# Layer-norm lo parts and sums of u moved to VectorE, the last token tile finished later, and layer norm ranked ahead of weight splits

## The chip, the core and the metric

The kernel runs on one core of a Trainium2 chip. The metric is the device time of one launch in microseconds (us). The core has five engines that each work through a fixed list of instructions in order: TensorE (matmuls and transposes; PE in the profile, its weight loads PEld), VectorE (DVE), ScalarE (ACT), GpSimd (POOL) and SyncE (SP, which issues the DMAs here). They wait for one another through semaphores.

## The reference, cut to what matters

One inference step of a two-layer backbone for 128 context tokens and 512 latent tokens of width 1024. Each layer has three sublayers, and each sublayer ends in a layer norm; the modulated input of the next one is u.

```python
def swiglu(u, lp, j):
    return (jax.nn.silu(u @ lp['ffn_w_gate'][j]) * (u @ lp['ffn_w_up'][j])) @ lp['ffn_w_down'][j]

def trunk_layer(x, cond, lp, ropes, ctx):
    mod = (jax.nn.silu(cond) @ lp['w_mod'] + lp['b_mod'])[:, None, :]
    sh1, sc1, g1, sh2, sc2, g2, sh3, sc3, g3 = jnp.split(mod, N_MOD, axis=-1)
    x = layer_norm(ALPHA * x + 0.5 * g1 * swiglu(x * (1 + sc1) + sh1, lp, 0), lp['ln_g'][0], lp['ln_b'][0])
    y, ctx_out = mixer(x * (1 + sc2) + sh2, lp, ropes, ctx)      # RG-LRU, GQA and MLA heads on one input projection
    x = layer_norm(ALPHA * x + g2 * y, lp['ln_g'][1], lp['ln_b'][1])
    x = layer_norm(ALPHA * x + 0.5 * g3 * swiglu(x * (1 + sc3) + sh3, lp, 1), lp['ln_g'][2], lp['ln_b'][2])
    return x, ctx_out
```

All is float32; D_FF is 2816.

## The kernel before

**Numbers as pairs.** A float32 matmul is made of three matmuls in the faster fp32r type: every operand is split into a hi part (a rounded copy, made by ScalarE) and a lo part (the rest, a subtraction). Weights are split as they come: `weight` returns a load and two splits, hi (L195, ScalarE) and lo (L200, VectorE). `mm3` (L537 to L539) issues the three matmuls.

**Phases.** The 640 tokens are five tiles of 128 (tile 0 is the context). The phases in order: FFN 0 of layer 0 (`ffn_steps`), mixer, FFN 1 (`ffn_fast`), then layer 1: FFN 0 (`ffn_fast`), mixer, FFN 1 (`ffn_fast`). So there are five layer ends inside the kernel and a last one at its end. The first phase, which computes u in another way, isn't touched by the change, except at its layer end.

**A layer end.** The last down projection (L832 or L1203 to L1205) or the output projection of the mixer goes tile by tile. VectorE multiplies each half tile from PSUM with the gate, adds it to x and takes the statistics (`ln_part`, L478). `end_tile` calls `ln_a` for the tile (aggregate L485, +eps L487, the power -0.5 on GpSimd L488, the offset L502, then the normalization in place, one part on ScalarE L506 and the rest on VectorE L508), and, one tile later, `modulate`, which calls `ln_b`: eight transposes on TensorE (L516), the evacuation with scale and shift into `uf` (L521 on VectorE, L523 on ScalarE), the hi part of u on ScalarE (L527) and its lo part on GpSimd (L529). The last tile's `ln_b` is kept in `after_q` and issued by `after_a`, which the next phase's `first` calls once the matmuls of its first weight on the first 384 tokens (24, tiles 0 to 2) are issued.

**The start of a fast FFN.** `first` of `ffn_fast` does block m = 0: gate on tokens 0 to 383, then `after_a`, up on the same tokens, gate and up on the other tokens. Blocks m = 1 and 2 follow in the same way, in halves of 320 tokens. Meanwhile `sums` forms the sums of quarters of u that the later blocks use (a Strassen scheme of seven products, L1091): eight additions hi + lo on GpSimd (`whole`, L990), then additions (L997, L1002, L1003, L1009) and splits (L985, L986) on VectorE and ScalarE. `third` follows, and hands PSUM over to the banks of the seven products, once the evacuations of block m = 2 (`hout`, L941, and `split_h`, L926) are through. `residual` (L2351, L2352) rescales x for the next sublayer at the same time, on VectorE.

**The order.** The framework plans each engine's list ahead of time: at each moment the instruction of the highest rank among those that are ready by its plan; rank is program order, and `high_priority(offset=n)` moves what is inside n places ahead (AHEAD is 100, SUMS is 200). On the chip the lists stand as planned. `run` issues a step's own splits before its body, and, between the pieces of its body, splits of the next steps: of the first `look` steps that have any, `cap` of them at most.

```python
            near = [todo[k] for k in range(i + 1, min(len(steps), i + 40)) if steps[k].splits][: s.look]
            cap = s.cap
            for more in s.body():
                cap += more or 0
                nxt = next((q for q in near if q), None)
                if nxt and cap and self.ahead and nxt[0].ready():
                    nxt.popleft()()
                    cap -= 1
```

A split is ready once its load has been issued; seven raw buffers (NR) limit how far loads run ahead. The steps of `tokens` (four column blocks of the mixer's input projection, two weights with four splits each) have a cap of 2; the last of them adds 2 in its body. Between them and their neighbours stand `proj` steps with two splits.

Of the kernel before, what the change touches and what calls it, by code (L numbers as in the profile page):

```python
# [18 lines left out]
P = 128  # L19
# [5 lines left out]
CUT = 384  # L25
# [44 lines left out]
LN_LAG = 1, 1  # L70
WOUT = (0,), (1,), (2, 3)
WCAP = 1
LOV = ()
FA = 1
FIN = ()
QP = 1
# [6 lines left out]
AHEAD = 100  # L83
# [5 lines left out]
def f(ap):  # L89
    return ap.bitcast(F32)  # L90
# [20 lines left out]
class Kern:  # L111
# [359 lines left out]
            self.gb.append(t)  # L471

    def ln_part(self, t, h, n):

        if h == 0:
            self.st[t] = self.tiny([P, 4, 6], "bnst", 6)[:, 0:n]
        w = D // n
        self.nc.vector.bn_stats(self.st[t][:, h, :], self.x[t][:, h * w : (h + 1) * w])  # L478

    def ln_a(self, t):  # L480

        nc = self.nc
        x = self.x[t]
        mv = self.tiny([P, 2], "bnmv", 3)
        nc.vector.bn_aggr(mv, self.st.pop(t))  # L485
        ve = self.tiny([P, 3], "bnve", 3)
        nc.vector.tensor_scalar_add(ve[:, 0:1], mv[:, 1:2], EPS)  # L487
        nc.gpsimd.tensor_tensor(out=ve[:, 1:2], in0=ve[:, 0:1], in1=self.mhalf[:, 0:1], op=ALU.pow)  # L488
        if self.next_mod is None and t == NT - 1:
            for h in range(2):  # L490
                cs = slice(h * 512, (h + 1) * 512)
                nc.vector.scalar_tensor_tensor(  # L492
                    x[:, cs], x[:, cs], mv[:, 0:1], self.gb[0][:, cs], op0=ALU.subtract, op1=ALU.mult
                )
            for h in range(2):
                cs = slice(h * 512, (h + 1) * 512)
                nc.vector.scalar_tensor_tensor(  # L497
                    x[:, cs], x[:, cs], ve[:, 1:2], self.gb[1][:, cs], op0=ALU.mult, op1=ALU.add
                )
                nc.sync.dma_start(out=self.O[1][0, (t - 1) * P : t * P, cs], in_=x[:, cs])  # L500
            return
        nc.vector.tensor_scalar(ve[:, 2:3], mv[:, 0:1], ve[:, 1:2], -1.0, op0=ALU.mult, op1=ALU.mult)  # L502
        c = NORM_ACT[self.ln_idx[1] != 1]
        if self.next_mod is None:
            c = D
        nc.scalar.activation(x[:, 0:c], x[:, 0:c], AF.Identity, bias=ve[:, 2:3], scale=ve[:, 1:2])  # L506
        if c < D:
            nc.vector.tensor_scalar(x[:, c:D], x[:, c:D], ve[:, 1:2], ve[:, 2:3], op0=ALU.mult, op1=ALU.add)  # L508

    def ln_b(self, x, t, sp, bp, uh, ul):  # L510

        nc = self.nc
        g = 1 if t == 0 else 0
        pt = self.p2().rearrange("p a (b c) -> p (a b) c", c=P)
        for k in range(KT):
            nc.tensor.transpose(pt[:, k, :], x[:, k * P : (k + 1) * P], self.ident)  # L516
        uf = self.pp.tile([P, KT, P], F32, tag="uf", bufs=1, name=self.nm("uf"))
        for k in range(KT):
            s1, s2 = sp[:, g, k : k + 1], bp[:, g, k : k + 1]
            if k % 4 < EVAC[self.ln_idx[1] != 1]:  # L520
                nc.vector.tensor_scalar(uf[:, k, :], pt[:, k, :], s1, s2, op0=ALU.mult, op1=ALU.add)  # L521
            else:
                nc.scalar.activation(uf[:, k, :], pt[:, k, :], AF.Identity, bias=s2, scale=s1)  # L523
        for h in range(2):
            d = uh[h][:, :, t * P : (t + 1) * P]
            v = uf[:, 4 * h : 4 * h + 4, :]
            nc.scalar.copy(d, v)  # L527
            e = nc.vector if (t, h) in LOV else nc.gpsimd
            e.tensor_sub(ul[h][:, :, t * P : (t + 1) * P], v, f(d))  # L529

    def u_alloc(self):
        return [self.U([P, 4, TOK]) for _ in range(2)], [self.U([P, 4, TOK]) for _ in range(2)]
# [350 lines left out]
    def ffn_fast(self, l, j, mods):  # L883
# [8 lines left out]
        nc, I = self.nc, self.I  # L892
        env = {}
# [10 lines left out]
        def T():  # L904
            return env["pool"].tile([P, 512], F32, tag="T", bufs=2, name=self.nm("t"))
# [24 lines left out]
        def plain(m):  # L930
            g, u = {}, {}
            gl, gsp = self.weight(view(I["ffn_w_gate"], m), [P, KT, P], g, self.W)
            ul, usp = self.weight(view(I["ffn_w_up"], m), [P, KT, P], u, self.W)

            def silu(cut):
                for a, b in self.chunks(g["s"], g["ps"], cut):
                    nc.scalar.activation(a, b, AF.Silu)

            def hout(cut):
                for a, b in self.chunks(g["s"], u["ps"], cut):  # L940
                    nc.vector.tensor_mul(a, a, b)  # L941
                split_h(m, g["s"])

            def first():
                env["cm"] = self.tc.tile_pool(name=f"ffn{l}{j}", bufs=1, reuse_waits="tile")
                env["pool"] = env["cm"].__enter__()
                g["ps"], u["ps"] = self.p2(), self.p2()
                g["s"] = B()
                yield from self.mtile(g["ps"], g, 0, CUT)
                self.hold = True  # L950
                self.after_a()
                yield from self.mtile(u["ps"], u, 0, CUT)
                yield from self.mtile(g["ps"], g, 1, CUT)
                silu(CUT)
                env["sums"] = sums()
                self.bg.append(env["sums"])
                yield from self.mtile(u["ps"], u, 1, CUT)
                hout(CUT)

            def gate():  # L960
                g["ps"] = self.p2()
                g["s"] = B()
                for c in range(2):
                    yield from self.mtile(g["ps"], g, c)
                silu(HALF)

            def up():
                u["ps"] = self.p2()
                for c in range(2):
                    yield from self.mtile(u["ps"], u, c)  # L970
                hout(HALF)

            if m == 0:
                return [Step([gl, ul], gsp + usp, first)]
            return [Step([gl], gsp, gate), Step([ul], usp, up)]


        def sums():
            uh, ul = self.uh, self.ul
            env["S"] = {i: (SB([P, 4, HALF]), SB([P, 4, HALF])) for i in (1, 2, 4)}  # L980
            env["s3"] = []

            def put(i, t, ks):
                hi, lo = env["S"][i]
                nc.scalar.copy(hi[:, ks], t)  # L985
                nc.vector.tensor_sub(lo[:, ks], t, f(hi[:, ks]))  # L986

            def whole(h, ts, ks):
                t = B().rearrange("p (k n) -> p k n", k=2)
                nc.gpsimd.tensor_add(t, f(uh[h][:, ks, ts]), f(ul[h][:, ks, ts]))  # L990
                return t

            for r in range(2):
                ks = slice(2 * r, 2 * r + 2)
                with self.tc.high_priority(offset=SUMS):
                    t21, t22 = whole(0, H1, ks), whole(1, H1, ks)
                    nc.vector.tensor_add(t22, t21, t22)  # L997
                yield
                with self.tc.high_priority(offset=SUMS):
                    t11 = whole(0, H0, ks)  # L1000
                    put(1, t22, ks)
                    nc.vector.tensor_sub(t21, t11, t21)  # L1002
                    nc.vector.tensor_sub(t11, t22, t11)  # L1003
                yield
                env["s3"].append((t21, ks))
                with self.tc.high_priority(offset=SUMS):
                    t12 = whole(1, H0, ks)
                    put(2, t11, ks)
                    nc.vector.tensor_sub(t12, t12, t11)  # L1009
                    put(4, t12, ks)  # L1010
                yield
# [168 lines left out]
        def down(ms, begin=False, last=False):  # L1180
            def body():
# [12 lines left out]
                for t in range(NT):  # L1194
                    x = acc[t]
                    ts = slice(t * P, (t + 1) * P)
                    for h in range(2):
                        pt = self.p1()
                        cs = slice(h * 512, (h + 1) * 512)
                        for i, m in enumerate(ms):  # L1200
                            hh, hl = hs[m]
                            d = dws[m]
# [3 lines left out]
                        if begin:  # L1206
                            with self.tc.high_priority(offset=AHEAD):
                                nc.scalar.copy(x[:, cs], pt)
                        elif last:
                            tt = T()  # L1210
                            nc.vector.tensor_mul(tt, pt, env["gate"][1 if t == 0 else 0][:, cs])
                            nc.vector.tensor_add(x[:, cs], x[:, cs], tt)
                            self.ln_part(t, h, 2)
                        else:
                            with self.tc.high_priority(offset=AHEAD):
                                nc.vector.tensor_add(x[:, cs], x[:, cs], pt)  # L1216
# [80 lines left out]
    def mixer_steps(self, l, mods):  # L1297
        nc, I, O = self.nc, self.I, self.O
        env = {}
# [796 lines left out]
        def tokens(c0, evac, post, pre=lambda: None, pairs=0):  # L2096
# [39 lines left out]
                post()  # L2136
                yield

            return Step(lds, sps, body, 2)

        def kv_evac(t, pt):
            if t == 0:
# [444 lines left out]
```

## Time and profile before

| | us |
|---|---|
| median of 3 runs (lowest to highest) | 2592.18 (2592.03 to 2599.52) |
| profiled execution, its own time | 2593.82 |
| profiled execution, span of the trace | 2592.0 |
| TensorE busy in it | 2470.4 |
| VectorE busy in it | 1887.8 |
| ScalarE busy in it | 1067.8 |
| GpSimd busy in it | 534.6 |

The span runs from the first to the last instruction of the profiled execution; the 1.8 us between it and that execution's time lie around it. Busy times are sums of what the engines execute; time in which an engine waits is idle. The granted clock of TensorE is given as a share of its full 2.4 GHz; over the whole execution it was 0.984.

### The profile page before, as it was taken

To read this page: it belongs to the slowest core of one execution; us is meant where nothing else is said; L and a number is where in the kernel's file an instruction comes from. 1 tells how busy PE (TensorE), PEld (TensorE's weight loads), DVE (VectorE), ACT (ScalarE), POOL (GpSimd) and SP (SyncE) were. 2 spreads that over 40 slices of the span, in tenths; PEclk is the share of its full clock that TensorE was granted. 3 is DMA by queue.
4 is the path that set the end of the run, shared out by engine and by line. 5 is a ranking of instruction groups with operands and counts; after the bars stand their busy time and mean duration, and the time that the engine had idled before them with its cause. 6 is when DMAs were issued, how large, how long until landed. Compare 5 with 4: busy or idle time off the path is not lost. (4 is left out here: it accounts for less than half of the span.)

```text
span 2592.0 us, 40008 instructions
## 1 busy us (share of the span) xinstructions
PE 2470.4 (95%) x15804; PEld 2220.3 (86%) x15804; DVE 1887.8 (73%) x3087; ACT 1067.8 (41%) x1882; POOL 534.6 (21%) x463
## 2 busy tenths in 40 slices
PE   7899999999999989999999999999989999999997
PEld 7689889989757989999888999988976798999986
DVE  4877768677754687777779777777785568777777
ACT  3212111246665434434353433434657534433432
POOL 2421211133622410000222000022363233000022
PEclk9999999999999999999999999999999999999999
DMA  8644446522223233333323333232331423333321
GB/s 271 211 147 146 131 129 205 155 68 78 93 88 104 73 113 100 99 113 96 109 87 112 103 97 114 91 109 76 99 117 48 135 60 112 106 90 106 121 91 49
DMA packets 271507, 288.54 MB, mean 111 GB/s; under 512 B 13548, under 2 KB 224088, under 8 KB 271320
## 3 DMA queue, kind: packets, MB, share of 16 engines
q1 hardware_dynamic: 271072, 285.91, 35.6%
q8 instruction: 124, 2.03, 0.3%
q14 instruction: 63, 0.52, 0.1%
q10 hardware_dynamic: 248, 0.08, 0.0%
HBM read 268.17 MB, written 16.21 MB: 110 GB/s over the span
## 5 line engine op out<-in xcount | busy, mean ns | idle before, releaser
L1091 PE MATMUL pb<-u,w 128*128 128x320 f32 x2736 | 422.1, 310 | 8.8 <-DVE b L941 7.2
L1091 PEld LDWEIGHTS pb<-u,w 128*128 128x128 f32 x2736 | 408.0, 188 | 11.7 <-DVE b L941 6.6
L537 PE MATMUL p<-u,w 128*128 128x320 f32 (+2 forms) x1104 | 349.3, 317 | 4.1 <-ACT uf L523 3.0
L539 PE MATMUL p<-u,w 128*128 128x320 f32 (+2 forms) x1104 | 346.4, 314 | 5.3 <-DVE w L200 5.3
L538 PE MATMUL p<-u,w 128*128 128x320 f32 (+2 forms) x1104 | 347.4, 315 | 3.3 <-POOL u L529 3.3
L1091 PE MATMUL pb<-s,w 128*128 128x320 f32 x2052 | 323.4, 311 | 4.5 <-DVE w L1067 4.0
L1091 PEld LDWEIGHTS pb<-s,w 128*128 128x128 f32 x2052 | 307.7, 189 | 6.8 <-DVE w L1067 4.5
L1063 ACT CAST w<-raw 128x512 fp32r<-128x512 f32 x399 | 240.2, 619 | 165.7 <-DVE raw L1059 110.3
L1067 DVE TENSOR_TENSOR w<-raw,w 128x512 fp32r<-128x512 f32 x399 | 271.7, 694 | 35.0 <-ACT w L1063 34.2
L195 ACT CAST dw<-raw 128x1024 fp32r<-128x1024 f32 x87 | 89.1, 1050 | 451.3 <-PE p L1204 264.9
L341 DVE SCALAR_TENSOR_TENSOR x<-raw,cst,x 128x512 f32<-128x512 f32 x308 | 235.2, 811 | 34.3 <-DMA raw<-in_w_mod 34.0
L1203 PE MATMUL p<-dw,b 128*128 128x512 f32 x630 | 250.0, 397 | 10.7 <-DVE x L1216 9.2
L1204 PE MATMUL p<-dw,b 128*128 128x512 f32 x630 | 246.2, 391 | 0.0
L1205 PE MATMUL p<-dw,b 128*128 128x512 f32 x630 | 245.9, 390 | 0.0
L537 PEld LDWEIGHTS p<-u,w 128*128 128x128 f32 x1104 | 212.0, 192 | 9.1 <-ACT uf L523 3.9
L539 PEld LDWEIGHTS p<-u,w 128*128 128x128 f32 x1104 | 211.7, 192 | 6.4 <-DVE w L200 6.4
L538 PEld LDWEIGHTS p<-u,w 128*128 128x128 f32 x1104 | 212.1, 192 | 5.4 <-POOL u L529 5.1
L195 ACT CAST w<-raw 128x1024 fp32r<-128x1024 f32 x100 | 105.0, 1050 | 245.5 <-PE p L538 176.7
L1216 DVE TENSOR_TENSOR x<-x,p 128x512 f32<-128x512 f32 x150 | 102.7, 685 | 111.4 <-PE p L1205 111.4
L1165 POOL TENSOR_SCALAR x<-x 128x1024 f32<-128x1024 f32 x6 | 6.9, 1143 | 813.5 <-DMA x<-gd 588.5
L200 DVE TENSOR_TENSOR w<-raw,w 128x1024 fp32r<-128x1024 f32 x100 | 126.9, 1271 | 56.4 <-ACT w L195 52.3
L1203 PEld LDWEIGHTS p<-dw,b 128*128 128x128 f32 x630 | 118.5, 188 | 46.1 <-DVE x L1216 20.5
(367 smaller groups left out, 4948.0 us busy)
## 6 DMA issues: line engine op xcount, KB each, us to landing
raw<-in_w_mod SPq DMA_DIRECT2D x132, 512.0 KB
raw<-in_ffn_w_gate SPq DMA_DIRECT2D x88, 512.0 KB
raw<-in_ffn_w_up SPq DMA_DIRECT2D x88, 512.0 KB
raw<-in_ffn_w_down SPq DMA_DIRECT2D x88, 512.0 KB
raw<-in_w_in SPq DMA_DIRECT2D x26, 512.0 KB
xd<-x SPq DMA_DIRECT2D x25, 512.0 KB
raw<-in_w_out SPq DMA_DIRECT2D x16, 512.0 KB
t<-xd SPq DMA_DIRECT2D x30, 256.0 KB
```

What stands on the lines that cost most here:

```text
L195: nc.scalar.copy(h, hold["raw"])
L200: nc.vector.tensor_sub(l, hold["raw"], f(hold["hi"]))
L341: e.scalar_tensor_tensor(acc[:, cs], hold["raw"][:, cs], c, acc[:, cs], op0=ALU.mult, op1=ALU.add)
L537: nc.tensor.matmul(out, lhsT=wh, rhs=xh, start=start, stop=False)
L538: nc.tensor.matmul(out, lhsT=wh, rhs=xl, start=False, stop=False)
L539: nc.tensor.matmul(out, lhsT=wl, rhs=xh, start=False, stop=stop)
L1063: nc.scalar.copy(w[:, 0], at(src))
L1067: nc.vector.tensor_sub(w[:, 1], at(src), f(w[:, 0]))
L1091: nc.tensor.matmul(out, lhsT=a1, rhs=b1, start=(start and k == 0 and i == 0), stop=(k == 3 and i == 2), skip_group_check=not start,)
L1203: nc.tensor.matmul(pt, lhsT=hh[:, ts], rhs=d["hi"][:, cs], start=(i == 0), stop=False)
L1204: nc.tensor.matmul(pt, lhsT=hh[:, ts], rhs=d["lo"][:, cs], start=False, stop=False)
L1205: nc.tensor.matmul(pt, lhsT=hl[:, ts], rhs=d["hi"][:, cs], start=False, stop=(i == len(ms) - 1))
```

## The change

Six edits:

1. `ln_b`: the lo parts of u (50 subtractions) are made by VectorE instead of GpSimd.
2. `whole` in `sums`: the 24 additions hi + lo are made by VectorE instead of GpSimd.
3. `ln_part`, `ln_a` and `ln_b` are issued under `high_priority(offset=AHEAD)`.
4. In the last down projection of `ffn_fast`, the multiplication with the gate and the addition to x are issued under the same rank.
5. `first` of `ffn_fast` issues the first half of up's matmuls on the first tokens (12 of 24) before `after_a`.
6. `tokens` steps look two steps ahead for splits instead of one.

```diff
@@ -471,6 +470,10 @@
     def ln_part(self, t, h, n):
+        with self.tc.high_priority(offset=AHEAD):
+            self.ln_part_(t, h, n)
+
+    def ln_part_(self, t, h, n):
...
     def ln_a(self, t):
+        with self.tc.high_priority(offset=AHEAD):
+            self.ln_a_(t)
+
+    def ln_a_(self, t):
...
     def ln_b(self, x, t, sp, bp, uh, ul):
+        with self.tc.high_priority(offset=AHEAD):
+            self.ln_b_(x, t, sp, bp, uh, ul)
+
+    def ln_b_(self, x, t, sp, bp, uh, ul):
...
             nc.scalar.copy(d, v)
-            e = nc.vector if (t, h) in LOV else nc.gpsimd
-            e.tensor_sub(ul[h][:, :, t * P : (t + 1) * P], v, f(d))
+            nc.vector.tensor_sub(ul[h][:, :, t * P : (t + 1) * P], v, f(d))
...
                 yield from self.mtile(g["ps"], g, 0, CUT)
                 self.hold = True
+                part = self.mtile(u["ps"], u, 0, CUT)
+                yield next(part)
                 self.after_a()
-                yield from self.mtile(u["ps"], u, 0, CUT)
+                yield from part
                 yield from self.mtile(g["ps"], g, 1, CUT)
...
             def whole(h, ts, ks):
                 t = B().rearrange("p (k n) -> p k n", k=2)
-                nc.gpsimd.tensor_add(t, f(uh[h][:, ks, ts]), f(ul[h][:, ks, ts]))
+                nc.vector.tensor_add(t, f(uh[h][:, ks, ts]), f(ul[h][:, ks, ts]))
                 return t
...
                         elif last:
-                            tt = T()
-                            nc.vector.tensor_mul(tt, pt, env["gate"][1 if t == 0 else 0][:, cs])
-                            nc.vector.tensor_add(x[:, cs], x[:, cs], tt)
+                            with self.tc.high_priority(offset=AHEAD):
+                                tt = T()
+                                nc.vector.tensor_mul(tt, pt, env["gate"][1 if t == 0 else 0][:, cs])
+                                nc.vector.tensor_add(x[:, cs], x[:, cs], tt)
                             self.ln_part(t, h, 2)
...
-            return Step(lds, sps, body, 2)
+            return Step(lds, sps, body, 2, look=2)
```

`LOV` was the empty tuple, and is gone.

## Rows read from the trace of the kernel before

**Rows 1.** The page, busy us of each engine, share of the span, instructions.

```profile
PE 2470.4 (95%) x15804; PEld 2220.3 (86%) x15804; DVE 1887.8 (73%) x3087; ACT 1067.8 (41%) x1882; POOL 534.6 (21%) x463
```

**Rows 2.** Windows: length, busy us of PE, PEld, DVE, ACT, POOL, then PEclk, DMA.

```profile
545.00:566.00 21.00, 16.86 (x85) 15.11 (x84) 14.72 (x49) 13.04 (x28) 8.86 (x12) 0.84 0.10 22
884.00:903.00 19.00, 14.58 (x81) 13.37 (x80) 10.67 (x22) 9.06 (x17) 12.79 (x8) 0.91 0.51 145
919.00:949.00 30.00, 23.16 (x135) 22.32 (x135) 29.60 (x45) 11.18 (x18) 0.00 (x0) 0.89 0.34 123
1337.00:1360.00 23.00, 18.49 (x101) 17.25 (x100) 14.05 (x24) 14.56 (x28) 11.22 (x10) 0.85 0.32 95
1374.00:1388.00 14.00, 10.08 (x59) 9.82 (x58) 14.00 (x18) 5.69 (x8) 0.65 (x1) 0.88 0.25 75
1792.00:1819.00 27.00, 22.34 (x125) 20.29 (x124) 17.33 (x51) 15.77 (x32) 9.10 (x12) 0.87 0.21 58
2127.00:2147.00 20.00, 16.68 (x100) 15.57 (x99) 13.12 (x24) 10.52 (x19) 11.38 (x8) 0.91 0.53 154
2162.00:2200.00 38.00, 32.49 (x195) 30.56 (x194) 37.36 (x60) 16.13 (x28) 0.00 (x0) 0.96 0.33 118
2549.00:2592.00 43.00, 28.17 (x121) 21.92 (x120) 35.21 (x58) 6.15 (x6) 14.98 (x13) 0.90 0.20 74
```

**Rows 3.** TensorE's waits, whole span: total us, times, longest us.

```profile
PE p L516 <- ACT x L506: 13.6, 6, 4.5
...
PE p L538 <- DVE w L200: 12.0, 8, 3.0
...
PE pb L1091 <- DVE b L941: 7.2, 2, 6.2
```

**Rows 4.** Lines L990, L529: duration ns min/median/max, first and last start us.

```profile
L990 POOL TENSOR_TENSOR b<-u,u x24: 1552/2156/2567, 901.4 to 2158.7; 128x640 f32<-128x640 f32 x24
L529 POOL TENSOR_TENSOR u<-uf,u x50: 1262/1291/3408, 532.0 to 2143.3; 128x512 fp32r<-128x512 f32 x50
```

**Rows 5.** VectorE's groups in 904:949: busy us, mean ns, idle before.

```profile
L986 DVE TENSOR_TENSOR s<-b,s 128x640 fp32r<-128x640 f32 x6 | 7.6, 1272 | 0.0
...
L200 DVE TENSOR_TENSOR w<-raw,w 128x1024 fp32r<-128x1024 f32 x3 | 5.0, 1666 | 5.6 <-ACT w L195 5.6
...
L997 DVE TENSOR_TENSOR b<-b,b 128x640 f32<-128x640 f32 x2 | 3.0, 1503 | 0.0
...
L1003 DVE TENSOR_TENSOR b<-b,b 128x640 f32<-128x640 f32 x2 | 2.7, 1334 | 0.0
L1002 DVE TENSOR_TENSOR b<-b,b 128x640 f32<-128x640 f32 x2 | 2.5, 1272 | 0.0
...
L1009 DVE TENSOR_TENSOR b<-b,b 128x640 f32<-128x640 f32 x2 | 1.6, 811 | 0.0
```

**Rows 6.** VectorE's timeline at a layer end: start us, us.

```profile
1338.21 1.27 DVE L508 TENSOR_SCALAR x<-x,bnve 128x512 f32<-128x512 f32 x1
...
1342.78 1.22 DVE L200 TENSOR_TENSOR w<-raw,w 128x1024 fp32r<-128x1024 f32 x1
...
1346.10 1.22 DVE L200 TENSOR_TENSOR dw<-raw,dw 128x1024 fp32r<-128x1024 f32 x1
...
1348.20 0.54 DVE L508 TENSOR_SCALAR x<-x,bnve 128x512 f32<-128x512 f32 x1
```

**Rows 7.** The page's group of VectorE's product-weight lo parts.

```profile
L1067 DVE TENSOR_TENSOR w<-raw,w 128x512 fp32r<-128x512 f32 x399 | 271.7, 694 | 35.0 <-ACT w L1063 34.2
```

**Rows 8.** TensorE's timeline at the same layer end, idle time in brackets.

```profile
1339.96 0.42 PE L537 MATMUL p<-u,w 128*128 128x384 f32 x1
...
1348.87 1.97 PE L516 MATMUL p<-ident,x 128*128 128x128 f32 x8 [4.50 <-ACT x L506]
```

**Rows 9.** SyncE's timeline in the first mixer, first loads of w_out.

```profile
748.75 11.18 SPq L190 DMA_DIRECT2D raw<-in_w_out x5
```

**Rows 10.** Line L1896, the attention scores: first and last start us.

```profile
L1896 PE MATMUL p<-x,b x448: 302/310/637, 664.6 to 2059.3; 128*128 128x320 f32 x86, 96*128 96x320 f32 x64
```

More of the change, by code (lines that the diff above doesn't have):

```diff
@@ L72 @@
 WCAP = 1
-LOV = ()
 FA = 1
```

## The prediction

> **What bounds the kernel now.** Read the page first: TensorE is busy for 2470.4 of 2592.0 us [rows 1], so what can be won is its 121.6 us of idle time and the time in which it runs at the lower clock. The view of what TensorE waits for says whom it waits for; the windows say where. In the windows the reader is to take two numbers per stretch: the length less PE busy (idle), and the length times (1 - PEclk), which is the time lost to the lower of the clock's two levels (1.2 instead of 2.4 GHz). Together they are the price of a place.
>
> The places that the diff touches fall in three sorts [rows 2], named by the phase that begins there:
> - Sums of u (fast FFNs): 919:949 idle 6.8 + clock 3.3 = 10.1; 1374:1388 3.9 + 1.7 = 5.6; 2162:2200 5.5 + 1.5 = 7.0. Sum 22.7 us. VectorE is busy 29.6 of 30.0, 14.0 of 14.0 and 37.4 of 38.0 us there: it sets the end.
> - Start of a fast FFN (layer norm, then `first`): 884:903 4.4 + 1.7 = 6.1; 1337:1360 4.5 + 3.5 = 8.0; 2127:2147 3.3 + 1.8 = 5.1. Sum 19.2 us.
> - Start of a mixer (layer norm, then the mixer's own `first`): 545:566 4.1 + 3.4 = 7.5; 1792:1819 4.7 + 3.5 = 8.2. Sum 15.7 us.
>
> So 57.6 us are at stake. Elsewhere TensorE works as before.
>
> **The change, part by part.**
>
> *Sums on VectorE.* 24 adds leave GpSimd, where the median takes 2.16 us [rows 4], eight for each fast FFN. Alone, a VectorE add of this shape takes 0.81 us (L1009) [rows 5]; the price added to VectorE's queue is 8 x 0.81 = 6.5 us per FFN. Against it stands what GpSimd does to VectorE while it runs them: in 904:949 the six L986 average 1.272 instead of 0.81 us, two L997 1.503, two L1003 1.334, two L1002 1.272 and three L200 1.666 instead of 1.22 us [rows 5, 6]. The excess is 6 x 0.46 + 2 x (0.69 + 0.52 + 0.46) + 3 x 0.44 = 7.4 us. So VectorE's queue is about 0.9 us shorter, not longer; and before the first L200 it was idle for 5.6 us, waiting for an earlier split [rows 5], while GpSimd's adds began at 901.4 [rows 4]. Six of the adds fit there (4.9 us). The queue behind runs 0.9 us earlier if none fits and 5.8 us earlier if they do. The end of the idle wait in 919:949 is L941, the evacuation that frees PSUM, 6.2 us late [rows 3]: saved are 0.9 to 5.8 us. I take 4.5 of idle and, since the gap then shrinks to about 1.7 us, 2.8 of the 3.3 of clock: 7.3 us. In 1374:1388 the wait is 3.9 us, less than 5.8, for a split L200 in the same queue: all 5.6 us. In 2162:2200 I take 5.0 of 7.0. Sum 17.9 us; bounds 3 x 0.9 = 2.7 and 22.7.
>
> The Trainium skill, "Perfetto Trace Analysis", section "Optimizing Scalar/DVE Operations", speaks against this part: if VectorE is saturated, moving work to GpSimd may make sense. By that alone the adds would go back onto a full engine, the third rival below. The same section adds that the two share an SBUF read port, so that such a move might not help; the rows of L986 and L997 bear that half out.
>
> *Lo parts of u on VectorE.* 50 subtractions of 128x512 leave GpSimd (median 1.29 us [rows 4]). The nearest VectorE row, L1067, has the same shape and mean 0.694 us [rows 7]: 1.4 us per token tile, two of them. In return L508, the normalization's VectorE half, takes 1.27 us beside GpSimd and 0.54 alone [rows 6]: 0.7 us back per tile. Net 0 (if a subtraction fills a bubble of the norm's chain) to 0.7 us more per tile. Only the lag at the last tile counts, for TensorE waits there alone (below). For the last tile itself the lo part is ready 0.6 us sooner, and VectorE's next evacuations no longer wait for GpSimd. I take 0 on balance, bounds -2 and +2 us per layer end.
>
> *Layer norm ahead of weight splits.* Priority decides between instructions that are ready together; it does not stop a 1.2 us split that has already started, nor one that fills a bubble while the norm's next step isn't ready. At 1342.78 to 1347.3 three splits (L200, 1.22 us each) stand between the last tile's statistics and its normalization [rows 6]. Bounds: 0 (all fill bubbles again) and 3.6 us (all go behind). I take 1.2, one split, where splits are in the way (the three FFN starts). The last FFN's `mul` and `add` gain the same rank; VectorE is busy 35.2 of the last 43.0 us [rows 2], and its queue has the same work before and after: 0, bounds -1.5 and +1.5.
>
> *The last token tile later.* `first` issues half of up's first chunk, 12 matmuls, ahead of the last tile's transposes. The 24 before them began at 1339.96 and ended 4.50 us before 1348.87, at 1344.37 [rows 8]: 0.184 us each, so 12 are 2.2 us of cover. The last tile's wait for its normalization is 4.5 us here; all six waits of this kind, which stand at the starts, come to 13.6 us [rows 3], so the others mean 1.8 us. What the move gives, it takes from the cover behind the transposes (12 instead of 24 matmuls for the evacuation): 0 to 2.2 us, and I take 0.5, as the lo part is faster. It issues no DMA; SyncE's queue keeps its order, and GpSimd's only loses work. With the split: 1337:1360 idle saved 2.2 + 1.2 - 0.5 = 2.9, leaving 1.6, and 2.6 of 3.5 clock: 5.5. At 884:903 and 2127:2147, 1.9 + 1.6 of clock each: 3.5. Sum 12.5 us; bounds 0 and 19.2. The mixers' starts keep their order: 0 and 1 us, bounds -4 and 6 together.
>
> *Splits two steps ahead.* `tokens` keeps its cap of two splits per step, and the next step's own queue (four or two) uses it up, so a second step is never reached. Only the last `tokens` step has a cap of four behind a step of two splits; the next weights with splits after it are w_out's, whose first loads are issued at 748.75, long after the attention that follows that step began at 664.6 [rows 9, 10], and a split needs its load. So 0: the mixers' waits for L200 (12.0 us in 8 waits [rows 3]) stay. Bounds 0 and -12.
>
> **Sum.** 17.9 + 12.5 + 1 = 31.4 us; I take off 1.4 for waits that were hidden behind the ones removed (a split or an evacuation next in VectorE's queue). 2593.8 - 30 = 2563.8 us for the profiled execution; the median of the runs is 1.6 us below that execution, so 2562 us.
>
> **Rivals.**
> - *Only the sums pay* (0.25). Splits fill the same bubbles and the subtractions take what L508 gives back. For it: VectorE's bubbles are real, and priority doesn't close them. Against: the extra 2.2 us of cover needs no priority. 2592.2 - 17.9 = 2574 us.
> - *Transposes too early* (0.06, slower). TensorE takes its instructions in a fixed order. With layer norm's rank its transposes may be ordered among the down projection's matmuls, at the point where the planner thinks the tile is normalized; if VectorE is late, all of TensorE stands. Place: 20 (five layer ends, tiles 0 to 3). Price at the lateness that the last tile shows now, 2 us as a mean: 40 us, 2562 + 40 = 2602. It decides from 1.5 us per tile on. Against: the lateness comes largely from VectorE beside GpSimd, which goes.
> - *VectorE too full* (0.04, slower). The moved adds stand in its queue with no relief: 3 x 6.5 = 19.5 us later, less the starts' 12.5: 2592.2 + 7 = 2599, and slower by more where the clock falls again. It decides if the L986 stay above 1.2 us with GpSimd idle.
> - *Nothing visible* (0.09). The lower bounds: sums 2.7, starts 0 to 3: 2587 us.
> - *Nearly all of it* (0.14). Both stages lose their gaps and half-speed stretches: 22.7 + 19.2 + 3 = 45 us, 2547.
> - The forecast, 2553 to 2570 us: 0.42.
>
> A measurement of this kernel tells 0.3%, 7.8 us, from no change. Faster: 0.42 + 0.25 + 0.14 = 0.81, and 0.01 of the fourth rival; same 0.08 of it and 0.01 of the slower ones; slower 0.09. The range that leaves out no more than 2 in 10 goes from just short of the fifth case, 2546, to between the first and fourth rival, 2584.
>
> **What would show it.** Right: L986, L997, L1002 and L1003 all at 0.81 us; no PE wait of over 2 us for L941 or L200 at the three sums, and PEclk of 1.0 there; the last tile's transposes at the FFN starts waiting under 2 us; the mixers' L200 waits unchanged. Wrong: PE waits for L506 or L508 at tiles 0 to 3; more time between the L508 of one token tile and the next than today, with L508 at 0.54; or the sums' waits still there with L986 at 0.81, which would mean that the queue's length and not its contention set them.

## The result, and the profile after

| | before | changed |
|---|---|---|
| first comparison, median of 4 runs each (us) | 2595.74 (2592.03 to 2599.52) | 2567.73 (2565.77 to 2570.72) |
| ratio, 95% interval | | 0.9893 [0.9871, 0.9915] |
| second comparison on another occasion (us) | 2598.57 (2593.67 to 2603.20) | 2569.57 (2566.62 to 2572.33) |
| ratio, 95% interval | | 0.9893 [0.9877, 0.9908] |
| profiled execution, own time / span (us) | 2593.82 / 2592.0 | 2566.97 / 2564.7 |
| granted clock over it | 0.984 | 0.991 |

The change makes the kernel 28 us faster. Line numbers moved: L516 became L527, L506 L513, L508 L515, L200 L199, L537 to L539 became L547 to L549, L990 L1002, L986 L998, L997 L1009, L1002 L1014, L1003 L1015, L1009 L1021, L941 L951, and the lo part L529 is L539, now on VectorE. First the page's busy times, which answer to [rows 1].

```profile
PE 2461.1 (96%) x15804; PEld 2209.1 (86%) x15804; DVE 1892.9 (74%) x3161; ACT 1069.1 (42%) x1882; POOL 414.3 (16%) x389
```

The span is 27.3 us shorter. TensorE's idle time fell from 121.6 to 103.6 us, 18.0 of the 27.3; the other 9.3 are busy time: the same 15804 matmuls ran less of their time at the lower clock (granted 0.991 instead of 0.984). GpSimd lost 74 instructions and 120 us, and VectorE, which took them over, is only 5.1 us busier. The trace says where the rest went: on VectorE the 74 last 53.6 us (50 of 0.68 and 24 of 0.82), but the durations of its other instructions fell by 36.6 us in sum, those of L508 by 7.6. The remaining difference is overlap of neighbouring instructions, which busy time counts once. Next the windows (columns as in [rows 2]) on the same eight places: three sums, three starts of a fast FFN, two starts of a mixer.

```profile
907.00:932.00 25.00, 25.00 (x171) 24.74 (x170) 23.83 (x33) 11.37 (x17) 0.00 (x0) 1.00 0.22 65
1361.00:1376.00 15.00, 15.00 (x104) 14.96 (x103) 15.00 (x22) 6.09 (x9) 0.00 (x0) 1.00 0.16 50
2145.00:2165.00 20.00, 20.00 (x135) 19.74 (x134) 19.45 (x32) 7.71 (x13) 0.00 (x0) 1.00 0.39 145
...
880.00:900.00 20.00, 18.14 (x126) 17.23 (x127) 17.51 (x40) 12.90 (x23) 1.10 (x2) 1.00 0.31 88
1325.00:1348.00 23.00, 19.79 (x114) 17.44 (x113) 19.81 (x38) 16.84 (x33) 1.41 (x2) 1.00 0.25 73
2110.00:2132.00 22.00, 20.27 (x138) 19.46 (x137) 19.73 (x37) 14.15 (x24) 1.40 (x1) 1.00 0.47 144
...
538.00:560.00 22.00, 19.90 (x108) 17.08 (x107) 19.71 (x57) 14.19 (x30) 2.78 (x7) 1.00 0.07 21
1784.00:1806.00 22.00, 20.15 (x133) 20.00 (x134) 16.67 (x50) 12.74 (x26) 3.78 (x3) 0.92 0.45 138
```

At the sums TensorE has no idle time left and the full clock, though VectorE is as full as before. At the starts 1.7 to 3.2 us of idle remain in each window, at full clock but for one. VectorE's groups during the first sums answer to [rows 5].

```profile
L1002 DVE TENSOR_TENSOR b<-u,u 128x640 f32<-128x640 f32 x8 | 6.2, 820 | 0.0
L998 DVE TENSOR_TENSOR s<-b,s 128x640 fp32r<-128x640 f32 x6 | 4.9, 820 | 0.0
...
L199 DVE TENSOR_TENSOR w<-raw,w 128x1024 fp32r<-128x1024 f32 x3 | 3.7, 1221 | 0.0
...
L1009 DVE TENSOR_TENSOR b<-b,b 128x640 f32<-128x640 f32 x2 | 1.6, 822 | 0.0
...
L1015 DVE TENSOR_TENSOR b<-b,b 128x640 f32<-128x640 f32 x2 | 1.6, 820 | 0.0
L1014 DVE TENSOR_TENSOR b<-b,b 128x640 f32<-128x640 f32 x2 | 1.6, 820 | 0.0
```

All at 0.82 us, where before they took 1.27 to 1.50, and the split is back at 1.22. TensorE's waits over the whole span answer to [rows 3].

```profile
PE p L527 <- ACT x L513: 11.9, 16, 2.3
PE p L548 <- DVE w L199: 10.6, 6, 3.0
...
PE p L548 <- DVE u L539: 3.7, 5, 1.4
...
PE p L547 <- ACT u L538: 2.9, 3, 1.6
```

The sums' wait for L941 is gone from the list. The transposes' waits for the normalization went from 6 to 16 in number and hardly fell in total. The waits of matmuls for u itself (hi part L538, lo part L539), 6.6 us, did not go either. Before, they were 3.3 us for GpSimd's lo part, 3.0 for the evacuation L523 and 0.8 for the hi part L527; the first of them:

```profile
PE p L538 <- POOL u L529: 3.3, 6, 1.0
```

So the starts did not go as forecast.

**Where the time went, place by place.** Each trace holds 15804 matmul records, so the time between two record numbers can be compared with the same stretch of before, wherever the same matmuls lie ahead of both ends. The table gives this difference in us, worked out from the start times of the records. A *projection* is what runs ahead of a start, the output projection of the mixer or a last down projection, up to the first matmul of the next phase (records 3379, 5705, 8307, 10907 and 13235); the sums are, for one, records 5850 to 6180. The kernels are those of the experiments below.

| place | sums only | lo only | rank only | later tile only | changed | changed, again | lo and sums, second time |
|---|---|---|---|---|---|---|---|
| three sums | -23.6 | -2.6 | +0.4 | -7.4 | -24.0 | -24.0 | -23.6 |
| projections ahead of the three FFN starts | 0.0 | +1.0 | +15.0 | 0.0 | +7.6 | +7.7 | +1.1 |
| three starts of a fast FFN | +0.5 | -5.2 | -9.4 | +6.9 | -10.7 | -8.7 | -5.0 |
| projections ahead of the two mixer starts | 0.0 | +2.0 | +7.0 | 0.0 | +3.5 | +3.6 | +2.1 |
| two starts of a mixer | -1.2 | -9.0 | -10.0 | -1.2 | -9.1 | -9.1 | -9.1 |
| all else | +3.8 | +5.4 | +3.0 | +3.7 | +5.3 | +3.0 | +3.2 |

The last line is positive in every column; the likely reason is that the profiled execution of before, at 2593.82, lies 3 to 5 us under the medians of 2596.6 to 2598.6 that its runs gave beside the experiments.

### The profile page after: what moved, and what is told of

It is laid out like the page before. It is cut to its first block, busy times and chain, and to the rows that moved or that the text cites. A ratio compares the mean times of both kernels' runs of the same rounds, so it can differ in the third digit from the quotient of the medians.

```text
span 2564.7 us, 39963 instructions
## 1 busy us (share of the span) xinstructions
PE 2461.1 (96%) x15804; PEld 2209.1 (86%) x15804; DVE 1892.9 (74%) x3161; ACT 1069.1 (42%) x1882; POOL 414.3 (16%) x389
## 5 line engine op out<-in xcount | busy, mean ns | idle before, releaser
L1103 PE MATMUL pb<-u,w 128*128 128x320 f32 x2736 | 420.5, 309 | 1.7 <-DVE b L1149 1.7
L1103 PEld LDWEIGHTS pb<-u,w 128*128 128x128 f32 x2736 | 406.7, 188 | 4.0 <-issue 2.4
L547 PE MATMUL p<-u,w 128*128 128x320 f32 (+2 forms) x1104 | 345.0, 313 | 3.2 <-ACT u L538 2.9
L548 PE MATMUL p<-u,w 128*128 128x320 f32 (+2 forms) x1104 | 343.7, 312 | 3.8 <-DVE u L539 3.7
L549 PE MATMUL p<-u,w 128*128 128x320 f32 (+2 forms) x1104 | 341.8, 311 | 0.0
L1103 PE MATMUL pb<-s,w 128*128 128x320 f32 x2052 | 322.1, 310 | 1.0 <-ACT b L1156 0.9
L1103 PEld LDWEIGHTS pb<-s,w 128*128 128x128 f32 x2052 | 306.0, 188 | 3.4 <-ACT b L1156 1.5
L547 PEld LDWEIGHTS p<-u,w 128*128 128x128 f32 x1104 | 208.4, 189 | 8.6 <-ACT u L538 3.9
L548 PEld LDWEIGHTS p<-u,w 128*128 128x128 f32 x1104 | 208.7, 189 | 5.5 <-DVE u L539 4.7
L549 PEld LDWEIGHTS p<-u,w 128*128 128x128 f32 x1104 | 208.3, 189 | 0.1
L199 DVE TENSOR_TENSOR w<-raw,w 128x1024 fp32r<-128x1024 f32 x100 | 124.9, 1249 | 35.0 <-ACT w L194 31.1
```

The costliest lines, as they stand in the source:

```text
L199: nc.vector.tensor_sub(l, hold["raw"], f(hold["hi"]))
L547: nc.tensor.matmul(out, lhsT=wh, rhs=xh, start=start, stop=False)
L548: nc.tensor.matmul(out, lhsT=wh, rhs=xl, start=False, stop=False)
L549: nc.tensor.matmul(out, lhsT=wl, rhs=xh, start=False, stop=stop)
L1103: nc.tensor.matmul(out, lhsT=a1, rhs=b1, start=(start and k == 0 and i == 0), stop=(k == 3 and i == 2), skip_group_check=not start,)
```

## The experiments

### One edit at a time

Each is the kernel before with one part of the change; the four ran on one chip, where before had a median of 2596.62 us.

**Sums only** (edit 2).

```diff
-                nc.gpsimd.tensor_add(t, f(uh[h][:, ks, ts]), f(ul[h][:, ks, ts]))
+                nc.vector.tensor_add(t, f(uh[h][:, ks, ts]), f(ul[h][:, ks, ts]))
```

> The kernel before with the sums of u alone moved to VectorE. Theory (the sums were late because GpSimd's additions are slow and slow VectorE's beside them): most of the whole change's gain, 20 to 23 us, so about 2572 us; the waits of the transposes for the sums' parts go, VectorE's reductions there fall from 1.27 to 1.5 us to about 0.81 us, and the starts of the layers stay as they were. Rival (the sums were late because the layer's order issues them late): at most 10 us, with waits of the transposes left at the three sums.

Measured: 2572.72 us, ratio 0.9913 [0.9898, 0.9927], 23.9 us faster; the three sums in the table give 23.6, and the starts hardly moved. The theory holds, with the size at the upper end.

**Lo parts only** (edit 1).

```diff
-            e = nc.vector if (t, h) in LOV else nc.gpsimd
-            e.tensor_sub(ul[h][:, :, t * P : (t + 1) * P], v, f(d))
+            nc.vector.tensor_sub(ul[h][:, :, t * P : (t + 1) * P], v, f(d))
```

> The kernel before with the lo parts alone on VectorE. Theory (the projections after a norm waited for GpSimd's subtraction behind the chain of the last token tile): 4 to 6 us, most of it at the two mixers' starts, about 2590 us. Rival (the norm's rank gave that, and the lo parts only change the engine): within 2 us of the kernel before.

Measured: 2581.75 us, ratio 0.9943 [0.9929, 0.9958], 14.9 us faster. Both expectations were too small: 7.0 us at the mixers' starts with their projections, as the theory had it, but also 4.2 at the FFN starts with theirs and 2.6 at the sums. The traces show two things that changed. The first is what GpSimd does to VectorE, here in before, at the first mixer's start: start, duration, engine, line. L1494 is a step on 128x4 elements in the mixer's preparation; two of VectorE's rows and the two GpSimd subtractions beside them:

```profile
556.31 1.21 DVE L1494 TENSOR_TENSOR spt<-spt 128x4 f32<-128x4 f32 x1
...
558.16 1.25 DVE L1494 TENSOR_TENSOR spt<-spt 128x4 f32<-128x4 f32 x1
...
556.24 1.26 POOL L529 TENSOR_TENSOR u<-uf,u 128x512 fp32r<-128x512 f32 x1 [2.52 <-DVE uf L521]
558.12 1.28 POOL L529 TENSOR_TENSOR u<-uf,u 128x512 fp32r<-128x512 f32 x1 [0.62 <-ACT u L527]
```

The same step where GpSimd does nothing, in the kernel with the lo parts on VectorE:

```profile
557.27 0.16 DVE L1493 TENSOR_TENSOR spt<-spt 128x4 f32<-128x4 f32 x1
```

An instruction of 0.16 us takes as long as the GpSimd subtraction that started just before it. It stood in VectorE's list ahead of an evacuation of the norm. The normalization step L508 suffered in the same way. First its line in before, then with the lo parts on VectorE: shortest, median and longest duration in ns.

```profile
L508 DVE TENSOR_SCALAR x<-x,bnve x25: 537/681/1368, 526.6 to 2134.7; 128x512 f32<-128x512 f32 x15, 128x768 f32<-128x768 f32 x10
```

```profile
L508 DVE TENSOR_SCALAR x<-x,bnve x25: 534/544/681, 528.4 to 2126.1; 128x512 f32<-128x512 f32 x15, 128x768 f32<-128x768 f32 x10
```

The second is the order. With other work on VectorE the framework plans the lists anew, and other instructions stand first. At the first mixer's start in before, TensorE's waits are these:

```profile
554.52 1.09 PE L516 MATMUL p<-ident,x 128*128 128x128 f32 x8 [1.69 <-ACT x L506]
557.45 0.69 PE L537 MATMUL p<-u,w 128*128 128x384 f32 x1 [1.83 <-ACT uf L523]
...
564.80 0.39 PE L538 MATMUL p<-u,w 128*128 128x256 f32 x1 [0.43 <-POOL u L529]
```

The two long steps have no part in the first two waits: what ended the second, an L523, started at 556.24, ahead of both. They can have a part only in the last, of 0.43 us. The longest wait is for the evacuation of tile 3, which stands in ScalarE's list behind the last tile's normalization (L506), itself 3.04 us late:

```profile
553.65 0.81 ACT L506 ACTIVATE x<-x,bnve 128x512 f32<-128x512 f32 x1 [3.04 <-DVE bnve L502]
554.37 1.14 ACT L523 ACTIVATE uf<-p,bp,sp 128x128 f32<-128x128 f32 x3
```

With the lo parts on VectorE the first half of that evacuation stands ahead of L506, this wait is gone, and the clock stays at 1.00 in the window, where it was 0.84 [rows 2]:

```profile
552.79 1.15 ACT L523 ACTIVATE uf<-p,bp,sp 128x128 f32<-128x128 f32 x3 [2.42 <-DVE uf L521]
...
556.02 0.81 ACT L506 ACTIVATE x<-x,bnve 128x512 f32<-128x512 f32 x1
```

```profile
547.00:568.00 21.00, 18.51 (x117) 16.72 (x116) 15.64 (x56) 13.86 (x31) 2.23 (x6) 1.00 0.15 47
```

The kernel with the rank only (below) has its lo parts still on GpSimd, and still VectorE steps of 1.15 and 1.28 us beside them, but its ScalarE list has the evacuation (551.98) ahead of the normalization (556.92) as well: it wins 10.0 us at the two mixers' starts, against 9.0 here, though it loses more in the projections ahead of them. At the second mixer's start GpSimd did cost TensorE time: two L1495 of 1.12 and 1.15 us delayed the last tile's evacuation, and matmuls waited 0.80 us for its hi part and 0.95 for GpSimd's lo part.

The second FFN start is mainly a matter of order too. In before, two splits, at 1344.94 and 1346.10, stand between the last tile's aggregate and its offset L502; with the lo parts on VectorE none does, and the transposes wait 1.96 us instead of 4.50 [rows 8]:

```profile
1344.09 0.20 DVE L485 BATCH_NORM_AGGREGATE bnmv<-bnst 128x2 f32<-128x12 f32 x1
1344.32 0.15 DVE L487 TENSOR_SCALAR bnve<-bnmv 128x1 f32<-128x1 f32 x1
1345.21 0.21 DVE L502 TENSOR_SCALAR bnve<-bnmv,bnve 128x1 f32<-128x1 f32 x1 [0.73 <-POOL bnve L488]
```

```profile
1346.32 1.97 PE L516 MATMUL p<-ident,x 128*128 128x128 f32 x8 [1.96 <-ACT x L506]
```

**Rank only** (edits 3 and 4).

```diff
     def ln_b(self, x, t, sp, bp, uh, ul):
+        with self.tc.high_priority(offset=AHEAD):
+            self.ln_b_(x, t, sp, bp, uh, ul)
...
```

and the same around `ln_part`, `ln_a` and the last `tensor_mul` and `tensor_add`.

> The kernel before with the rank of the norm's work and of the last addition alone. Theory (the rank also brings the transposes of token tiles 0 to 3 forward into the output projection, where each waits 0.4 to 0.9 us for its norm): some 3 us lost at each of the ends before an FFN, little won at the starts, in all 0 to 8 us slower. Rival (the rank clears the norm's chain of weight splits at the starts): 5 us faster.

Measured: 2603.34 us, ratio 1.0034 [1.002, 1.0048], 6.7 us slower. TensorE's waits over the span (L528 is the transposes, L514 the normalization, L1103 the products, L953 the evacuation at the sums):

```profile
PE p L528 <- ACT x L514: 21.3, 22, 4.2
...
PE pb L1103 <- DVE b L953: 12.3, 3, 8.1
```

and two of the 22 in its timeline, in the middle of the last output projection, where TensorE had no such wait before:

```profile
2108.78 1.09 PE L528 MATMUL p<-ident,x 128*128 128x128 f32 x8 [0.73 <-ACT x L514]
...
2116.96 1.09 PE L528 MATMUL p<-ident,x 128*128 128x128 f32 x8 [1.40 <-ACT x L514]
```

The five projections lose 22.0 us (15.0 and 7.0), and the five starts win 19.4 back (9.4 and 10.0). The theory holds on the total and on the place of the loss: TensorE runs its list in order, and the rank puts the transposes of the early tiles into it ahead of matmuls that were ready. That little is won at the starts does not hold; there the rank does what the rival said.

**Later tile only** (edit 5).

```diff
+                part = self.mtile(u["ps"], u, 0, CUT)
+                yield next(part)
                 self.after_a()
-                yield from self.mtile(u["ps"], u, 0, CUT)
+                yield from part
```

> The kernel before with the last token tile finished one matmul group later, alone. Theory (2.2 us of cover for the last tile's norm at each of three FFN starts): 6 to 10 us faster. Rival (the last tile's transposes only wait later, for the same chain or for GpSimd's lo part): within 2 us of the kernel before.

Measured: 2596.49 us over 10 runs, ratio 0.9998 [0.9989, 1.0008]. The rival holds. TensorE's timeline at the second start:

```profile
1349.44 1.09 PE L516 MATMUL p<-ident,x 128*128 128x128 f32 x8 [2.08 <-DVE dw L200]
...
1354.97 0.79 PE L537 MATMUL p<-u,w 128*128 128x256 f32 x2 [3.74 <-ACT u L527]
1356.32 0.58 PE L538 MATMUL p<-u,w 128*128 128x256 f32 x1 [0.56 <-POOL u L529]
```

The transposes wait 2.08 us where it was 4.50 [rows 8], a gain of 2.4; but the matmuls behind them, which need the last tile's u, now wait 3.74 us for its hi part and 0.56 for its lo part. The 12 matmuls that were put ahead had covered just that. The table shows the FFN starts 6.9 us longer and the sums 7.4 shorter.

**Edit 6 alone** gives each of the five engines the same list of instructions as before, one for one; it was not run.

### Is it the engine at work, or the length of its additions?

**Beside the sums.** The changed kernel, with a GpSimd addition beside each addition of the sums.

```diff
+            z = T().rearrange("p (k n) -> p k n", k=2)
...
                 nc.vector.tensor_add(t, f(uh[h][:, ks, ts]), f(ul[h][:, ks, ts]))
+                cs = slice(ts.start, ts.start + 256)
+                nc.gpsimd.tensor_add(z, f(uh[h][:, ks, cs]), f(ul[h][:, ks, cs]))
```

> The changed kernel with a GpSimd addition of 512 elements per partition beside each of the eight additions of the sums of u, into a scratch tile that nobody reads. Theory (the sums were late because the parts on GpSimd took 2 us each ahead of VectorE's): VectorE's additions there rise from 0.81 us, but the time stays within 4 us of the changed kernel (2566 to 2572 us). Rival (the sums were late because GpSimd at work slows VectorE): half or more of the 24 us comes back, 2578 us or more.

Measured: 2583.42 us, ratio 0.995 [0.9933, 0.9967] to a before of 2597.99: 14.6 us faster than before, where the changed kernel is 28 to 29. The rival holds: additions that nobody waits for take half of the gain away, 14 of the 24 us that stand at the sums. How much of the other 10 is that the sums' own parts, on GpSimd, came late is not separated; the additions beside are also shorter, 512 elements instead of 640. The timeline at the first sums, GpSimd's row ahead of VectorE's:

```profile
904.47 9.09 POOL L1005 TENSOR_TENSOR t<-u,u 128x512 f32<-128x512 f32 x5
...
903.16 1.91 DVE L1003 TENSOR_TENSOR b<-u,u 128x640 f32<-128x640 f32 x1
905.00 1.92 DVE L1012 TENSOR_TENSOR b<-b,b 128x640 f32<-128x640 f32 x1
906.84 0.54 DVE L951 TENSOR_TENSOR b<-b,p 128x384 f32<-128x384 f32 x1
907.30 1.45 DVE L1017 TENSOR_TENSOR b<-b,b 128x640 f32<-128x640 f32 x1
908.68 1.92 DVE L999 TENSOR_TENSOR s<-b,s 128x640 fp32r<-128x640 f32 x1
910.52 1.92 DVE L1018 TENSOR_TENSOR b<-b,b 128x640 f32<-128x640 f32 x1
...
912.69 1.95 DVE L199 TENSOR_TENSOR w<-raw,w 128x1024 fp32r<-128x1024 f32 x1
914.57 0.81 DVE L999 TENSOR_TENSOR s<-b,s 128x640 fp32r<-128x640 f32 x1
```

While GpSimd runs, the two engines take turns: most of VectorE's rows start 1.84 us apart, and GpSimd's five take 1.82 each. The first addition or split to start after GpSimd has ended, at 913.56, takes 0.81 again. L951, whose second input is in PSUM (p), is not held up. And the waits at the second and third sums in this kernel:

```profile
PE p L549 <- DVE w L199: 3.6, 1, 3.6
```

```profile
PE p L549 <- DVE w L199: 3.7, 1, 3.7
```

It is the split at the end of VectorE's queue that comes late.

The Trainium skill, "SBUF — State Buffer", section "SBUF: two separate sides", says that VectorE and GpSimd share one pair of ports, held by one instruction at a time, and that a VectorE instruction with two SBUF inputs waits for it in full, beside a GpSimd one that reads SBUF. The rows agree: 0.16 us against 1.21 to 1.25, and 0.81 against 1.91 to 1.92.

**Beside the lo parts.** The kernel with lo parts only, with three GpSimd subtractions beside each.

```diff
             nc.vector.tensor_sub(ul[h][:, :, t * P : (t + 1) * P], v, f(d))
+            z = self.pp.tile([P, 4, 48], F32, tag="Z", bufs=1, name=self.nm("z"))
+            for c in (0, 48, 80):
+                nc.gpsimd.tensor_sub(z, f(d[:, :, c : c + 48]), f(d[:, :, c : c + 48]))
```

> The lo parts alone on VectorE, and beside each of them three GpSimd subtractions of 192 elements per partition into a scratch tile that nobody reads. Theory (the lo parts on GpSimd cost most of their 15 us because they slowed VectorE's steps of the norm, such as the 0.54 us step at 1.25 us): most of the gain is lost, 2590 us or more. Rival (TensorE waited for the lo parts themselves, or the evacuations for the tile that GpSimd still read): the gain stays, 2586 us or less.

Measured: 2609.68 us, ratio 1.0044 [1.0028, 1.006]: all of the gain is lost, and 11 us more. But this does not settle what the theory asked. GpSimd's timeline shows the power of the norm (L488) behind one of the added subtractions (L531), which came from the tile before:

```profile
1337.38 0.95 POOL L531 TENSOR_TENSOR z<-u 128x192 f32<-128x192 f32 x1 [2.61 <-ACT u L527]
1338.29 0.55 POOL L488 TENSOR_TENSOR bnve<-bnve,mhalf 128x1 f32<-128x1 f32 x1
```

So the experiment delays the norm's chain in a way that the kernel before did not at this start. How the lo parts' 15 us divide between what GpSimd does to VectorE, the waits for the lo parts themselves (3.3 us in before) and the new order of the lists stays open; the rows above show all three at work.

### Which of the other edits are worth having?

These four ran in two groups; a ratio is to the before of the same chip.

**Without the rank** (edits 1, 2 and 5).

```diff
-        with self.tc.high_priority(offset=AHEAD):
-            self.ln_b_(x, t, sp, bp, uh, ul)
...
```

> The changed kernel without the rank of the norm's work and of the last addition. Theory (the rank costs some 7 us whatever else is changed, since it puts the transposes of tiles 0 to 3 in front of matmuls that were ready): the gains of sums and lo parts add up, 2556 to 2561 us. Rival (with the lo parts on VectorE the rank is what keeps them ahead of weight splits): 2567 us or more.

Measured: 2566.50 us, 0.9877 [0.9863, 0.9892]. This is above the theory's range and half a us short of the rival's: the gains of 23.9 and 14.9 us do not add up to 38.8, and the interval overlaps that of the changed kernel, so beside the other edits the rank's 6.7 us are not told apart from nothing.

**Rank for the last tile's transposes only.**

```diff
     def ln_b(self, x, t, sp, bp, uh, ul):
+        if t < NT - 1:
+            return self.ln_b_(x, t, sp, bp, uh, ul)
         with self.tc.high_priority(offset=AHEAD):
```

> The changed kernel with the rank of the transposes and evacuations kept for the last token tile alone; statistics and normalisation keep theirs. Theory (the transposes brought forward are the whole cost of the rank): 2555 to 2560 us, no slower than without any rank. Rival (the ranked statistics and additions delay the output projection's evacuations): 2563 us or more.

Measured: 2566.88 us, 0.9878 [0.9863, 0.9892]: slower than the theory's range, the same as without any rank. The time is the rival's; whether its mechanism is, was not looked at.

**Lo parts and sums, nothing else** (edits 1 and 2, twice), and the **changed kernel again** beside the second.

> The kernel before with the lo parts and the sums on VectorE, and nothing else. Theory (finishing the last tile later pays only once its lo part is off GpSimd): 4 to 6 us slower than the same kernel with the later last tile, 2562 to 2565 us. Rival (the cover is taken back behind the transposes in either case): within 2 us of it.

> Lo parts and sums on VectorE and nothing else, a second time: 2562 to 2567 us, and what this is under the changed kernel beside it is the price of its other edits.

> The changed kernel itself, beside the next one on the same chip. Theory (the rank still costs some 2 to 4 us in the changed kernel): 2 to 5 us slower than lo parts and sums alone. Rival (what the rank loses in the output projection it wins back at the starts): within 2 us of them.

Measured: 2564.78 us, 0.9872 [0.9857, 0.9887], within 2 us of the kernel without the rank, so the later tile is worth nothing here either. The second time 2560.99 us, 0.9858 [0.9844, 0.9871], against 2569.57, 0.9893 [0.9877, 0.9908], for the changed kernel: 8.6 us less, and the intervals do not overlap. So two edits of the six give more than all six: by 8.6 us beside it, and by 5 in the first run, on another chip, where the intervals overlap. The transposes' waits in the second run:

```profile
PE p L516 <- ACT x L506: 13.6, 10, 2.9
```

They wait as long in total as in [rows 3], in 10 waits instead of 6. In the profiles the two spans differ by only 3.7 us (2564.4 and 2560.7), and the places of the table account for it: all six edits lose 8.1 us more in the projections and win 3.7 more at the FFN starts. The other 4.9 us lie between the profiled executions and the medians: that of the changed kernel was the fastest of its four (2566.62), that of the other kernel the slowest of its four (2562.97).

**Lo parts, sums, and the rank on the last tile's chain.**

```diff
+        with self.tc.high_priority(offset=AHEAD if t == NT - 1 else 0):
+            self.ln_a_(t)
...
```

> Lo parts and sums on VectorE, and the rank for the last token tile alone (statistics, normalisation, transposes, evacuations and the last addition). Theory (the rank is worth something only on the last tile's chain): 2 to 6 us faster than lo parts and sums alone, 2558 to 2562 us. Rival (weight splits fill VectorE whatever the rank, since the chain's steps aren't ready when they are taken up): within 2 us of them.

Measured: 2565.43 us, 0.9872 [0.9859, 0.9886], 4.4 us more than without, with overlapping intervals. The theory is out; nothing was won on the last tile by rank.

## Why the prediction was right, and where its steps were not

The forecast was 2562 us, the result 2567.7 and 2569.6, inside the likeliest case's range of 2553 to 2570. The sum of 30 us met 28, but with its terms wrong on both sides: in the changed kernel the sums gave some 6 us and the mixers' starts 4.6 more than forecast, the FFN starts, with their projections, 9 to 12 less. That they cancelled was luck.

- **Sums, 17.9 us predicted, 23.6 to 24.0 measured.** The mechanism was right: GpSimd beside VectorE, which the additions beside the sums showed for more than half of it, and all the groups named came down to 0.82 us. The size was not: I left 5 of the 22.7 us at stake behind, in case the queue didn't get ahead far enough. All of it went.
- **Lo parts, 0 predicted, 15 us measured.** This is the step that failed: "I take 0 on balance, bounds -2 and +2 us per layer end", 10 us at most over five ends. I set L508's 0.7 us against two subtractions of 0.69 on VectorE and called it even. I had the row of one instruction that GpSimd held up and did not look for others: small steps of the mixer's own preparation, 0.16 us long, stood for 1.2 us each. And I took the lists as they were. The move had them planned anew, and at the first mixer's start and the second FFN start that, not the held-up steps, took TensorE's longest waits away.
- **Mixers' starts, 1 us predicted, 5.6 measured**: 9.1 won, 3.5 lost in the projections ahead. "The mixers' starts keep their order" holds for the program, not for the lists. Their waits for L200 nearly stayed, as said (12.0 to 10.6 us).
- **Starts of the fast FFNs, 12.5 us predicted; 8.7 to 10.7 won, 7.6 to 7.7 of it lost in the projections just ahead.** That loss stands in no term of the sum. Alone, the later tile is worth nothing and the rank costs 6.7 us. I wrote that the move takes 0 to 2.2 us from the cover behind the transposes and took 0.5; it takes all. Lo parts and sums by themselves win 3.9 us at the same places. Of the three splits that I read as standing between the last tile's statistics and its normalization, the first stands ahead of its last statistics; the other two are in between.
- **Splits two steps ahead, 0**: right, by the lists.
- **Transposes too early** (a rival of 0.06). Its mechanism is real: alone the rank makes 22 waits out of 6, and the changed kernel has 16. Its price was set too high: it needs 1.5 us of lateness per tile, and in the changed kernel the 16 waits mean 0.74 us.
- **VectorE too full** (0.04). The condition was L986 above 1.2 us with GpSimd idle; they took 0.82. But there is little room: at the first sums in the kernel with additions beside, the rows shown are 4 x 1.1 + 0.6 + 0.7 = 5.7 us longer, and at the second and third sums it is the splits behind such rows that TensorE waits for, 3.6 and 3.7 us.
- **The signs.** The groups at 0.81 us: yes. No waits over 2 us at the sums, clock 1.0: yes. Waits of the last tile's transposes under 2 us at the FFN starts: yes, but the next matmuls took over, 1.6 us for the hi part and 1.4 for the lo part of u, which I did not name. Waits at tiles 0 to 3, named as a sign of being wrong: there, and small.

## What to carry to other kernels

Before pricing a move between VectorE and GpSimd, list every VectorE group's shortest and longest duration beside GpSimd's timeline: what the busy engine loses can weigh as much as what the moved work costs. Where a scheduler plans the lists, compare each engine's order before and after as well, before a gain is put down to contention. Matmuls that cover a wait ahead of an instruction are taken from the cover behind it, so look at what the next matmul needs before moving them. A rank that brings work forward on the late engine also brings its consumers forward on TensorE, where they stand in front of work that was ready.

## What the runs showed of the hardware

A small VectorE instruction with two inputs in SBUF lasts as long as the GpSimd instruction beside it: 128x4 elements took 1.21 and 1.25 us beside GpSimd's 1.26 and 1.28, and 0.16 alone. One of VectorE's inputs in PSUM was enough to be spared (0.54 us for 128x384 in the middle of GpSimd's additions, 0.55 in the changed kernel with GpSimd idle). One tensor in SBUF as the only tensor input was not: L508 took 1.27 us instead of 0.54 [rows 6], and L1495, on 128x4 elements, 1.12 and 1.15 us instead of 0.17 at the second mixer's start. It works the other way as well: the norm's power L488 on GpSimd took 1.40 us instead of 0.55 when a split of 1.22 us had just started on VectorE (before, 1346.32 and 1346.10).
